# Gate projections of seven heads in a stage of their own, as seven products with eight sums

## The chip, the cores and the metric

The kernel runs on one core of a Trainium2 chip. The core has a matrix engine (TensorE, PE in the profile, with its weight loads as PEld), three engines for elementwise work (VectorE or DVE, ScalarE or ACT, GpSimd or POOL), a queue engine (SyncE or SP) and 16 DMA engines. All run their own instruction streams in order and wait for each other by semaphores. The metric is the device time of one execution in microseconds.

## The reference, cut to what matters

A block for 1024 tokens of width 1024: a normalization, one wide projection, a recurrent mixer with 8 heads of 128 (the part that is changed), an attention with 16 heads, two output projections that are gated and mixed, and a feed-forward part.

```python
h = rms_norm(x, norm1_gain[layer])
proj = h @ w_in[layer]
hq, hf, hi, hg, sq, sk, sv, ga, gb = split_cols(proj, IN_SPLITS)
o_hg = hgrn2_mixer(hq, hf, hi, lower_bounds[layer])
o_hg = rms_norm(o_hg, hg_out_norm[layer]).reshape(b, s, HG_WIDTH)
o_hg = o_hg * jax.nn.sigmoid(hg.astype(jnp.float32))
```

and in the mixer, for each head and in chunks of 64 tokens:

```python
f = lb + (1.0 - lb) * jax.nn.sigmoid(f_raw.astype(jnp.float32))
log_f = jnp.log(f)
k = 1.0 - f
...
cum = jnp.cumsum(g_c, axis=-2)
o = scores(q, k, cum) @ v + (q * exp(cum)) @ state
state = exp(last) * state + (k * exp(last - cum)).T @ v
```

The last two lines are shortened to their meaning. The two gate projections of a head are hf (the gate f) and hg (the output gate), each a product of a 1024 x 128 slice of w_in with h.

## The kernel before

**Exact products.** Each float32 operand is split into a rounded part and a rest (hi and lo, in a 32-bit format that PE reads in one pass). `mm3` (L158 to L162) makes one product of three matmuls: hi x hi, hi x lo, lo x hi. h is kept transposed as `hT[half][hi or lo]`, features on the partitions, 512 tokens in each half.

**Projections.** `proj_t` (through `chain`, L164) gives a 128-column slice of a projection, transposed: for each half, 8 steps over K, each an `mm3` with 512 columns, into a bank of the pool pd, and then an evacuation. `proj_v` gives tiles of v with 256-wide matmuls. Weights come by `load_w` (L121 to L141): a load on SP's queue into wr, a cast to wh on ACT, the negated copy to wl on ACT, and an accumulating DMA on POOL's queue that adds wr; for the first five loads the difference is made on DVE instead. wr has two buffers, wh and wl three each. `block` has the next two blocks loaded ahead.

**Start.** x comes in tiles of 128 tokens; `norm_x` normalizes a tile, `turn_x` transposes it on PE and splits it to hT. `first_head` gives the projections f, g and q of head 0: the first half of the tokens as quarters that are woven into the turning of the tiles (cut0, cut1), the second half behind it (rest). Then come the projections of v for heads 0 and 1 (v0).

**Recurrent stage.** For each of 8 heads, `hg_head` returns `prep` and a list of own steps with costs: `base` (scores in blocks of 4), `across`, four levels of scores (`level_prep` on DVE, POOL and ACT, `level` on PE and a predicated copy on DVE), `turn`, `state`, `read` and `norm`. `hg_gates` (L410 to L425) turns the projected f and g into gates: two Sigmoids on ACT, a table load before and one after, f = lb + (1 - lb) x on DVE, k on POOL, Ln on ACT, and a scan on DVE. The filling of head h is the projections f and g of head h+1 (`hg_fg`, with the gates behind them), q of head h+1, and two tiles of v; that of head 7 is three projections of other gates (`gate_steps`). `weave` fixes the order on PE: it lets filling go ahead by the cost `lead`, and spreads the rest over the own steps in proportion to their costs. PE's order is that of the program text; the other engines' orders are made by the planner from readiness and priority.

**Later stages.** The attention, the output projections and the feed-forward part follow. The last two use seven products in place of eight: both operands are cut in 2 x 2 quarters, sums and differences of quarters are made (`A_STEPS`, `B_STEPS`), and seven products of quarters are added up in banks and in SBUF. In the feed-forward part `a_prep` makes the weights' side six products ahead.

Of the kernel before, what the change touches and what calls it, by code (L numbers as in the profile page):

```python
# [41 lines left out]
def hybrid_block(ctx, tc, x, norm1_gain, w_in, lb_logits, hg_out_norm, sb_q_norm, sb_k_norm,  # L42
# [75 lines left out]
    d_x1 = dp.tile([NT, P, D], F32, name="d_x1")  # L118
    d_act = dp.tile([3, NF // 2, P, HS], F32, name="d_act")
# [99 lines left out]
    hg = hgctx.enter_context(tc.tile_pool(name="hg", bufs=2))  # L219
# [3 lines left out]
    g1 = hg.tile([P, D], F32, tag="sc", bufs=1, name="g1")  # L223
# [7 lines left out]
    xts = {}  # L231

    def fetch_x(t):
        xts[t] = hg.tile([P, D], F32, tag=("kv", "q")[t % 2], name="xt")
        nc.sync.dma_start(xts[t], x[t * P:(t + 1) * P, :])
        if t == 0:
            nc.sync.dma_start(g1, norm1_gain.partition_broadcast(P).rearrange("p a d -> p (a d)"))

    def norm_x(t):
        xt = xts.pop(t)  # L240
        hn = hg.tile([P, D], F32, tag=("c", "fv")[t % 2], name="hn")
        ss = mp.tile([P, 1], F32, tag="ss", bufs=8, name="ss")
        sq = nc.scalar.activation(hg.tile([P, D], F32, tag="ke", bufs=1, name="scr"), xt, AF.Square, accum_out=ss)
# [12 lines left out]
    def turn_x(t):  # L256
        hn, half, c0 = hns.pop(t), t // 4, (t % 4) * P
        for g in range(2):
            tp = pbank(("pt", "pz")[t % 2])
            for j in range(4):  # L260
                k = 4 * g + j
                nc.tensor.transpose(tp[:, j * P:(j + 1) * P], hn[:, k * P:(k + 1) * P], ident)
            last["hT"] = split_to(hT[half][0][:, 4 * g:4 * g + 4, c0:c0 + P],
                     hT[half][1][:, 4 * g:4 * g + 4, c0:c0 + P], tp.rearrange("p (k c) -> p k c", k=4))
# [8 lines left out]
    def small_vectors():  # L273
# [13 lines left out]
        nc.scalar.activation(lbt[:, 1:3, :], lbt[:, 1:3, :], AF.Exp)  # L287
# [85 lines left out]

    def first_head():
        d, cuts, rest = hd[0], ([], []), []
        for c0, n in ((1024, "fv"), (3072, "sg"), (0, "q")):
            w, evac = in_block(c0), copy_half(d, n)
            last.setdefault("w0", w)
            for a, b in zip(cuts, quarters(w, evac, n == "fv")):
                a.extend(b)  # L380
            rest += proj_t(w, evac, (1,))
            if n == "sg":
                rest.append((0.0, lambda: hg_gates(0)))
        return *cuts, rest

# [3 lines left out]
    def hg_v(h, tiles=range(4)):  # L389
        get = in_block(2048 + h * P, 256)  # L390
# [19 lines left out]

    def hg_gates(h):
        d = hd[h]
        fv, sg = d["fv"], d["sg"]
        with tc.high_priority():
            s1 = nc.scalar.activation(fv, fv, AF.Sigmoid)
# [3 lines left out]
        nc.vector.tensor_scalar(fv, fv, oml[:, h:h + 1], lb[:, h:h + 1], op0=ALU.mult, op1=ALU.add)  # L419
# [4 lines left out]
        order(nc.scalar.activation(c, fv, AF.Ln, bias=tiny), pre)  # L424
        nc.vector.tensor_tensor_scan(c, rmask, c, initial=0.0, op0=ALU.mult, op1=ALU.add)  # L425

    def hg_head(h):
# [5 lines left out]
        def prep():  # L433
            if h % 2 == 0:
# [3 lines left out]
            kb = e["kb"] = hg.tile([P, S], F32, tag="kl", name="kb")  # L438
            qb = e["qb"] = hg.tile([P, S], F32, tag="kl", name="qb")
# [6 lines left out]
            nc.vector.tensor_mul(kb, kb, kv)  # L446
# [6 lines left out]
            nc.vector.tensor_mul(ke, ke, kv)  # L453
# [60 lines left out]
        def level_prep(li):  # L514
            L = LEVELS[li]
            kq = hg.tile([P, 2, HS], F32, tag="kl", name="kq")
# [16 lines left out]
        def level(li):  # L533
# [3 lines left out]
            for a in range(NT // 2):  # L537
                sl = slice(a * P, (a + 1) * P)
                nc.tensor.matmul(ps[:, sl], kq[:, 0, sl], kq[:, 1, sl], start=True, stop=True)
            nc.vector.copy_predicated(bl(e["sc"], L)[:, :, 1, :],  # L540
                                      lmask[:, li, :].rearrange("p (b l) -> p b l", l=L),
                                      ps.rearrange("p (b l) -> p b l", l=L))
# [14 lines left out]
        def norm(half):  # L557
# [14 lines left out]
            (0.5, lambda: turn(0)),  # L572
            (1.257, lambda: turn(1)),
            (2.053, lambda: (level(1), level_prep(3))),
            (0.9, lambda: state(0)),
            (0.7, lambda: state(1)),
            (1.7, lambda: level(2)),
            (2.397, lambda: level(3)),
            (1.6, lambda: read(0)),
            (4.5, lambda: read(1)),  # L580
            (3.0, lambda: norm(0)),
            (0.45, lambda: norm(1)),
# [18 lines left out]
    v0 = hg_v(0)  # L601
# [22 lines left out]
    weave([(1.0, lambda t=t: turn_x(t)) for t in range(4, 8)], cut1, lead=3.429)  # L624
    hg_constants()
    small_vectors()
# [277 lines left out]
    def run(steps):  # L904
        for _, f in steps:
            f()

    A_STEPS = {5: (21, 21, 22, ALU.add), 6: (21, 21, 11, ALU.subtract), 7: (11, 22, 21, ALU.subtract),
               3: (12, 12, 21, ALU.subtract)}
    A_SRC = {1: 11, 2: 12, 5: 21, 6: 21, 7: 11, 3: 12, 4: 22}
    B_STEPS = {5: (11, 12, 11, ALU.subtract), 6: (11, 22, 11, ALU.subtract), 7: (12, 22, 12, ALU.subtract),
               4: (21, 21, 11, ALU.subtract)}
    B_SRC = {1: 11, 2: 21, 5: 11, 6: 11, 7: 12, 3: 22, 4: 21}
    INTO = {1: 11, 2: 11, 5: 22, 6: 12, 7: 22, 3: 12, 4: 21}
    OPENS, CHAIN = (1, 2, 5), (1, 6, 7, 4)
    FIRST, FINAL = (1, 5, 6, 4), (2, 7, 3, 4)

    def sum_step(e, steps, m, raw):
        if m in steps:
            to, a, b, op = steps[m]
            e.tensor_tensor(raw(to), raw(a), raw(b), op=op)  # L924

    def split(e, src, hi, lo):
        nc.scalar.copy(hi, src)  # L927
        e.tensor_sub(lo, src, hi.bitcast(F32))  # L928

    def chain_mm(ps, lhs, rhs, m, k, nk):  # L930
        mm3(ps, lhs, rhs, m in OPENS and k == 0, k == nk - 1, m not in OPENS)

# [233 lines left out]
    a_ops = {}  # L1166

    def a_prep(n):
        f, m = a_order[n]
        if m == 1:  # L1170
            load_raw(f)
        if m == 2:
            load_raw(f + 1)
        raw = lambda q: raws[f][q // 10 - 1][:, 4 * (q % 10) - 4:4 * (q % 10), :]
# [212 lines left out]
```

## Time and profile before

| | us |
|---|---|
| median of 3 runs (lowest, highest) | 2033.01 (2032.94, 2033.84) |
| the profiled execution | 2032.44 |
| its span, first to last instruction | 2030.6 |
| scan of head 0, of head 7 (L425) | 56.3, 460.0 |
| last predicated copy of head 7 (L540) | 500.0 |
| last store of the recurrence (L565) | 519.8 |

The scans of heads 0 and 7 lie 403.7 us apart, 57.7 us a head. The profile comes from one execution; its times are compared with each other and with its own 2032.44 us. In its rows a line such as "L342 DVE COPY fv<-pd 128x512 x2 | 1.4, 688 | 3.3 <-PE pd L162 3.3" means: line 342, engine, operation, tile written and tile read, shape, count, busy time in us, mean of one in ns, idle time of the engine ahead of it and what ended that. Rows of a timeline begin with the start and the duration.

### The profile page before, as it was taken

Reading aid. Unit: us, or ns where it says so; the run is one execution under the profiler, and the core shown is the slowest. Engines: PE = TensorE matmul, PEld = TensorE weight load, DVE = VectorE, ACT = ScalarE, POOL = GpSimd, SP = SyncE. Lnnn points to the kernel's source line nnn. Section 1 sums busy time; section 2 is a strip of 40 time slices with the busy share of each in tenths; the row PEclk is TensorE's granted clock in tenths of the full one; section 3 lists DMA queues with packets and bytes.
Section 4 is the critical chain, followed back from the end, with each engine's and each line's share of the span. In section 5 each row is a group of like instructions: output and inputs, shape, how many; then the busy total and the mean of one; then the engine's idle time right before and its main releaser. Section 6 shows DMA issues by size and latency. Waiting matters only on the chain.

```text
span 2030.6 us, 29534 instructions
## 1 busy us (share of the span) xinstructions
PE 2013.3 (99%) x11047; PEld 1727.5 (85%) x11047; DVE 1463.5 (72%) x2263; ACT 1131.6 (56%) x1889; POOL 322.1 (16%) x445
## 2 busy tenths in 40 slices
PE   9999999999999999999999999998999999999999
PEld 8988888888888988988988888887888888888887
DVE  6455666557277787787888598999766666568975
ACT  5455655455477777877877465458333333334443
POOL 1233323323231332232231000000000000000000
PEclk9999999999999999999999999999999999999999
DMA  4444434444555454444454644512322222266031
GB/s 166 115 110 109 115 94 125 113 127 104 132 114 115 97 127 114 99 108 113 104 118 112 229 170 162 182 49 98 103 81 86 83 81 65 78 221 221 30 114 42
DMA packets 204511, 234.74 MB, mean 116 GB/s; under 512 B 11416, under 2 KB 141904, under 8 KB 204368
## 3 DMA queue, kind: packets, MB, share of 16 engines
q1 hardware_dynamic: 181584, 185.01, 29.2%
q0 software_dynamic: 15632, 42.48, 12.1%
q10 hardware_dynamic: 7152, 5.37, 0.8%
q8 instruction: 87, 1.43, 0.3%
q14 instruction: 56, 0.46, 0.1%
HBM read 137.65 MB, written 42.21 MB: 89 GB/s over the span
## 4 chain that ended last, share of the span: by engine, by line
PE 86%; DVE 9%; ACT 1%; issue 1%; DMA 1%; POOL 0%; SPq 0%; DVEq 0%; ACTq 0%; POOLq 0%
PE pd L160 19%; PE pd L162 18%; PE pd L161 18%; PE pt L807 3%; PE pt L161 3%; PE pt L160 3%; PE pt L162 3%; DVE u L924 2%; PE po L824 2%; DVE u L928 2%; PE po L823 2%; PE pz L762 2%; PE pz L763 2%; PE po L160 2%; PE po L162 2%; PE po L161 2%
## 5 line engine op out<-in xcount | busy, mean ns | idle before, releaser
L160 PE MATMUL pd<-hT,wh 128*128 128x512 f32 (+1 forms) x912 | 368.6, 404 | 0.0
L162 PE MATMUL pd<-hT,wl 128*128 128x512 f32 (+1 forms) x912 | 352.7, 387 | 0.1
L161 PE MATMUL pd<-hT,wh 128*128 128x512 f32 (+1 forms) x912 | 352.4, 386 | 0.0
L927 ACT CAST wh<-u 128x512 fp32r<-128x512 f32 (+1 forms) x280 | 183.6, 684 | 227.0 <-PE po L162 86.6
L162 PEld LDWEIGHTS pd<-hT,wl 128*128 128x128 f32 x912 | 171.3, 188 | 36.6 <-DVE wl L138 0.3
L160 PE MATMUL pd<-u,wh 128*128 128x512 f32 x496 | 194.0, 391 | 1.5 <-ACT c L1235 0.7
L161 PE MATMUL pd<-u,wh 128*128 128x512 f32 x496 | 193.3, 390 | 0.2 <-DVE u L928 0.2
L160 PEld LDWEIGHTS pd<-hT,wh 128*128 128x128 f32 x912 | 172.0, 189 | 23.8
L161 PEld LDWEIGHTS pd<-hT,wh 128*128 128x128 f32 x912 | 172.2, 189 | 23.4 <-DVE hT L210 0.2
L928 DVE TENSOR_TENSOR wl<-u,wh 128x512 fp32r<-128x512 f32 (+1 forms) x196 | 150.3, 800 | 47.4 <-ACT wh L927 45.0
L774 DVE TENSOR_TENSOR_SCAN kp<-kp,dsel 128x512 f32<-128x512 f32 (+3 forms) x128 | 122.6, 958 | 36.6 <-ACT kp L767 36.0
L160 PE MATMUL pd<-wh,hT 128*128 128x256 f32 x512 | 148.0, 289 | 0.0
L162 PE MATMUL pd<-wh,hT 128*128 128x256 f32 x512 | 144.7, 283 | 0.0
L161 PE MATMUL pd<-wl,hT 128*128 128x256 f32 x512 | 144.6, 282 | 0.0
L767 ACT ACTIVATE kp<-pz,rq 128x128 f32<-128x128 f32 (+2 forms) x192 | 114.1, 594 | 44.0 <-PE pz L763 33.7
L162 PE MATMUL pd<-u,wh 128*128 128x512 f32 x352 | 137.0, 389 | 0.0
L924 DVE TENSOR_TENSOR u<-u,u 128x512 f32<-128x512 f32 (+1 forms) x152 | 124.3, 851 | 12.6 <-DMA u<-d_ohg 7.9
L810 DVE TENSOR_TENSOR tl<-pt,th 128x512 fp32r<-128x512 f32 (+1 forms) x160 | 100.1, 626 | 34.1 <-ACT th L809 33.7
L781 DVE TENSOR_TENSOR a<-a,kp 128x128 f32<-128x128 f32 (+2 forms) x192 | 109.7, 572 | 17.8 <-ACT a L767 3.4
L767 ACT ACTIVATE a<-pz,rq 128x128 f32<-128x128 f32 (+2 forms) x192 | 114.2, 595 | 7.2 <-PE pt L807 7.2
L160 PEld LDWEIGHTS pd<-u,wh 128*128 128x128 f32 x496 | 93.1, 188 | 21.7 <-ACT c L1235 1.1
L161 PEld LDWEIGHTS pd<-u,wh 128*128 128x128 f32 x496 | 93.2, 188 | 19.8 <-DVE u L928 0.9
(266 smaller groups left out, 4885.9 us busy)
## 6 DMA issues: line engine op xcount, KB each, us to landing
wr<-in_w_in SPq DMA_DIRECT2D x78, 512.0 KB, 4.0
wl<-wr POOLq DMA_DIRECT2D x73, 512.0 KB, 4.7
u<-in_w_ffn_in SPq DMA_DIRECT2D x24, 512.0 KB, 5.8
wr<-in_w_ffn_in SPq DMA_DIRECT2D x20, 512.0 KB, 3.9
u<-in_w_ffn_out SPq DMA_DIRECT2D x10, 1024.0 KB, 6.6
d_act<-c SPq DMA_DIRECT2D x33, 256.0 KB, 2.2
u<-d_act SPq DMA_DIRECT2D x8, 1024.0 KB, 13.3
qh<-qh SPq DMA_DIRECT2D x48, 128.0 KB, 2.3
```

Of the source, the lines that this page charges most:

```text
L160: nc.tensor.matmul(ps, lh, rh, start=start, stop=False, skip_group_check=adds)
L161: nc.tensor.matmul(ps, lh, rl, start=False, stop=False, skip_group_check=adds)
L162: nc.tensor.matmul(ps, ll, rh, start=False, stop=stop, skip_group_check=adds)
L762: nc.tensor.matmul(ps[:, :n], qhi[:, qs], kk[:, k0:k0 + n], start=True, stop=False)
L767: last["sig"] = [nc.scalar.activation(t[:, 0:w], ps[:, 0:w], AF.Sigmoid, scale=rq[:, n_, col:col + 1]) for n_, t in enumerate((kp, a))]
L774: nc.vector.tensor_tensor_scan(rev, rev, dsel[:, HS - w:][:, ::-1], initial=0.0, op0=ALU.mult, op1=ALU.max)
L781: nc.vector.tensor_mul(a[:, 0:w], a[:, 0:w], kp[:, 1:w + 1])
L807: nc.tensor.transpose(tp[:, s * P:(s + 1) * P], a[:, b * P:(b + 1) * P], ident)
L810: nc.vector.tensor_sub(tl[:, c0:], tp[:, c0:], th[:, c0:].bitcast(F32))
L924: e.tensor_tensor(raw(to), raw(a), raw(b), op=op)
L927: nc.scalar.copy(hi, src)
L928: e.tensor_sub(lo, src, hi.bitcast(F32))
```

## The change

The projections f and g of heads 1 to 7 leave the recurrent stage. They are made ahead of it in a stage of their own. For each head the weights (columns of f and of g as the two halves of the output, two halves of K) and h (two halves of K, two of the tokens) are cut in quarters, and seven products of 128 x 512 x 512 give the four quarters of the result. The sums on h's side are made once for all heads; those on the weights' side once for each head. The results go through Sigmoid, those of f through their scale and bound, and are stored to DRAM (d_fg). The recurrent stage loads them back (`hg_load`). Its filling is now q and v alone, heads 6 and 7 get one and two of the other gate projections, the own steps' order and costs are other ones, and there is a buffer count of 4 for kl. A class that was the feed-forward part's loop (`Pairs`) serves both stages.

```diff
+    class Pairs:
+        def prep(self, n):
+            f, m = self.order[n]
+            self.before(f, m)
+            raw = lambda q: self.raws[f][q // 10 - 1][:, 4 * (q % 10) - 4:4 * (q % 10), :]
+            both = wp.tile([P, 2, 4, P], F32R, tag=("wh", "wl")[n % 2], name="wh")
+            sum_step(nc.vector, A_STEPS, m, raw)
+            split(nc.vector, raw(A_SRC[m]), both[:, 0], both[:, 1])
+            self.ops[f, m] = both
+            self.after(f, m)
...
+        def step(self, n, k):
...
+            if k == 0:
+                self.ahead(n + 6)
...
+            chain_mm(ps, (w[:, 0, k, :], w[:, 1, k, :]), (bh[:, k, :], bl_[:, k, :]), m, k, 4)
+            if k == 3:
+                del self.ops[f, m]
+                self.done(f, m, ps)
...
+            last["hT"] = split_to(hT[half][0][cut], hT[half][1][cut], tp)
+            nc.scalar.copy(h_raw[q][:, :, c0:c0 + P], tp)
...
-    def hg_fg(h):
-        d = hd[h]
-        f, g = in_block(1024 + h * P), in_block(3072 + h * P)
-        return proj_t(f, copy_half(d, "fv")) + proj_t(g, copy_half(d, "sg")) + [(0.0, lambda: hg_gates(h))]
...
+    def to_gate(h, i, half, dst, src):
+        last["sig0"] = nc.scalar.activation(dst, src, AF.Sigmoid)
+        order(last["sig0"], last["rs", NT - 1], last["lb"])
+        if i == 0:
+            nc.vector.tensor_scalar(dst, dst, oml[:, h:h + 1], lb[:, h:h + 1], op0=ALU.mult, op1=ALU.add)
+        nc.sync.dma_start(d_fg[i][h][:, half * HS:(half + 1) * HS], dst)
...
+    h_sums = [lambda: h_sum(11, 12, 11), lambda: h_sum(12, 22, 12), lambda: h_sum(22, 22, 11), lambda: h_split(5, 11),
+              lambda: h_split(6, 22), lambda: h_sum(22, 21, 22), lambda: h_split(7, 12), lambda: h_split(4, 22)]
...
+    def hg_load(h):
+        d = hd[h]
+        for i, name in enumerate(("fv", "sg")):
+            d[name] = hg.tile([P, S], F32, tag=name, bufs=i + 1, name=name)
+            nc.sync.dma_start(d[name], d_fg[i][h])
...
     def hg_gates(h):
         d = hd[h]
-        fv, sg = d["fv"], d["sg"]
-        with tc.high_priority():
-            s1 = nc.scalar.activation(fv, fv, AF.Sigmoid)
-            order(s1, last[id(d), "sg"])
-            s2 = nc.scalar.activation(sg, sg, AF.Sigmoid)
-            pre = exp_ln_tables(s1, s2)
-        nc.vector.tensor_scalar(fv, fv, oml[:, h:h + 1], lb[:, h:h + 1], op0=ALU.mult, op1=ALU.add)
+        fv = d["fv"]
...
-            nc.vector.tensor_mul(kb, kb, kv)
+            order(nc.vector.tensor_mul(kb, kb, kv), *last.get("own", ()))
...
-            (0.86, lambda: (base(0), load_v(h) if h % 2 == 0 else None)),
-            (2.463, lambda: (base(1), level_prep(0))),
-            (2.075, lambda: (across(), level_prep(1))),
-            (2.243, lambda: (level(0), level_prep(2))),
...
+            (0.86, lambda: (base(0), load_v(h) if h % 2 == 0 else None, level_prep(0),)),
+            (2.46, lambda: (base(1), level_prep(1),)),
+            (5.60, lambda: (across(), level_prep(2),)),
+            (2.24, lambda: (level(0), level_prep(3),)),
...
-    weave([], rest + v0)
+    for i, (_, f) in enumerate(rest):
+        f()
+        if i % 3 == 2 and i < 14:
+            h_sums.pop(0)()
+        if i % 8 == 7:
+            pairs0.ahead(2 * (i // 8 + 1))
+    n0 = len(pairs0.order)
+    for n in range(n0):
+        if n == n0 - 5:
+            get = in_block(2048, 256)
+            get()
+            v0 = [hg_v(0, tiles, get) for tiles in ((0, 1), (2, 3))]
+        weave([], pairs0.steps(n))
+        if h_sums:
+            h_sums.pop(0)()
+    s0ctx.close()
+    hg = hgctx.enter_context(tc.tile_pool(name="hg", bufs=2, reuse_waits="tile"))
+    last["tables"] = [exp_ln_tables(last["sig0"])]
+    hg_load(0)
+    hg_gates(0)
+    weave([], v0[0])
+    prep, own = hg_head(0)
+    prep()
+    weave([], v0[1])
...
     for h in range(NH):
-        prep, own = hg_head(h)
-        prep()
         if h < NH - 1:
-            fill = hg_fg(h + 1) + hg_q(h + 1)
+            fill = hg_q(h + 1) + [(0.0, lambda: hg_gates(h + 1))]
+            if h == NH - 2:
+                fill += gate_steps(1)
             if h < NH - 2:
                 fill += hg_v(h + 1, (2, 3)) if h % 2 else hg_v(h + 2, (0, 1))
         else:
-            fill = gate_steps(3)
-        weave(own, fill, lead=6.109)
+            fill = gate_steps(2)
+        load_blocks()
+        if h > 0:
+            prep, own = hg_head(h)
+            prep()
+        if h < NH - 1:
+            hg_load(h + 1)
+        weave(own, fill, lead=5.53)
```

`h_sum` makes a difference of two quarters of h on DVE in two pieces of 128 x 1024, `h_split` a cast on ACT and a difference on DVE of such a quarter. `pair_done` copies the first part of a quarter of the result from its bank on ACT, adds the second on DVE, and passes it to `to_gate`. `pair_raw(f)` loads the weights of one head, 512 KB for f and 512 KB for g.

More of the change, by code (lines that the diff above doesn't have):

```diff
@@ new lines, in hybrid_block, with sum_step, split, chain_mm @@
+    OPENS, CHAIN = (1, 2, 5), (1, 6, 7, 4)
+    FIRST, FINAL = (1, 5, 6, 4), (2, 7, 3, 4)
+    def sum_step(e, steps, m, raw):
+        if m in steps:
+            to, a, b, op = steps[m]
+            e.tensor_tensor(raw(to), raw(a), raw(b), op=op)
+    def split(e, src, hi, lo):
+        nc.scalar.copy(hi, src)
+        e.tensor_sub(lo, src, hi.bitcast(F32))
+    def chain_mm(ps, lhs, rhs, m, k, nk):
+        mm3(ps, lhs, rhs, m in OPENS and k == 0, k == nk - 1, m not in OPENS)
+    class Pairs:
+        def __init__(self, order, raws, bop, before, after, done):
+            self.order, self.raws, self.bop = order, raws, bop
+            self.before, self.after, self.done = before, after, done
+            self.ops, self.banks, self.ready = {}, {}, 0
+        def prep(self, n):
[7 more added lines that the diff above has]
+            self.after(f, m)
+        def ahead(self, upto):
+            while self.ready < min(upto, len(self.order)):
+                self.prep(self.ready)
+                self.ready += 1
+        def step(self, n, k):
+            f, m = self.order[n]
+            key = f, "p" if m in CHAIN else "t"
+            if k == 0:
+                self.ahead(n + 6)
+                if m in OPENS:
+                    self.banks[key] = dbank() if m == 1 else pbank("po", 1) if m == 2 else pbank("pt")
+            ps, w = self.banks[key], self.ops[f, m]
+            bh, bl_ = self.bop[m]
+            chain_mm(ps, (w[:, 0, k, :], w[:, 1, k, :]), (bh[:, k, :], bl_[:, k, :]), m, k, 4)
+            if k == 3:
+                del self.ops[f, m]
+                self.done(f, m, ps)
+        def steps(self, n):
+            return [(0.65, lambda k=k: self.step(n, k)) for k in range(4)]
@@ new lines, in piece, with evac, go @@
+    def piece():
+        return s0.tile([P, HS], F32, tag="c", bufs=6, name="c")
+    postponed = []
+    def first_head():
+        cuts, rest = ([], []), []
+        def evac(i):
+            def go(half, ps):
+                c = piece()
+                if i == 2:
+                    nc.vector.tensor_copy(c, ps)
+                    nc.sync.dma_start(d_q[:, half * HS:(half + 1) * HS], c)
+                elif half == 1:
+                    to_gate(0, i, half, c, ps)
+                else:
+                    nc.vector.tensor_copy(c, ps)
+                    postponed.append(lambda: to_gate(0, i, half, c, c))
+            return go
+        for i, c0 in enumerate((1024, 3072, 0)):
+            w = in_block(c0)
@@ L386, in hg_q, with pair_order, hg_v @@
+    def pair_order(n_pairs, ahead):
+        order = [(f, m) for f in range(ahead) for m in (1, 2)]
+        for f in range(n_pairs):
+            n = [(f + 1, m) for m in (1, 2)] if ahead <= f + 1 < n_pairs else []
+            order += [(f, 5), (f, 6)] + n[:1] + [(f, 7)] + n[1:] + [(f, 3), (f, 4)]
+        return order
+    pairs0 = Pairs(pair_order(NH - 1, 2), raws0, hop, lambda f, m: None,
+                   lambda f, m: pair_raw(f + 2) if m == 4 else None, pair_done)
     def hg_q(h):
         return proj_t(in_block(h * P), copy_half(hd[h], "q"))
-    def hg_v(h, tiles=range(4)):
-        get = in_block(2048 + h * P, 256)
+    def hg_v(h, tiles=range(4), get=None):
+        get = get or in_block(2048 + h * P, 256)
@@ L906, in run @@
             f()
[L911 to L931, printed above, removed]
     def four_banks(m):
@@ L1318, in hybrid_block @@
             load_w_out(11, 0, unit2)
-        run(ffn_in(n))
+        run(ffn.steps(n))
     for i, u in ((1, unit1), (2, unit1)):
```

188 lines of the change are left out of this document (112 added, 76 removed).

## The prediction

> **What bounds the kernel now.** I read the page's busy shares and slices first, then the busy times in stretches of the span, then the waits of PE, and last the groups of one head.
>
> ```profile
> span 2030.6 us, 29534 instructions
> PE 2013.3 (99%) x11047; PEld 1727.5 (85%) x11047; DVE 1463.5 (72%) x2263; ACT 1131.6 (56%) x1889; POOL 322.1 (16%) x445
> PE   9999999999999999999999999998999999999999
> DVE  6455666557277787787888598999766666568975
> PE pt L1122 <- DVE hn L1118: 5.5, 1, 5.5
> PE pz L539 <- DVE kq L529: 1.1, 1, 1.1
> ```
>
> PE has work in every slice, and its list of waits holds two above 1.4 us in the whole span; neither falls in the stage that the change empties, except the second, in head 7. So PE's issue bounds the kernel nearly everywhere, and a matmul removed is worth its issue interval, not its printed duration: matmuls overlap in the pipeline. The interval is read where nothing but 512-wide matmuls runs, and from the first and last of a run of 256-wide ones.
>
> ```profile
> core 0: us, PE busy (x) PEld busy (x) DVE busy (x) ACT busy (x) POOL busy (x), PEclk, DMA share, GB/s
> 1600.00:1700.00 100.00, 100.00 (x443) 82.84 (x442) 63.90 (x96) 36.77 (x63) 0.00 (x0) 1.00 0.24 72
> 287.80:345.50 57.70, 57.70 (x362) 50.93 (x362) 35.26 (x54) 31.48 (x44) 18.02 (x18) 1.00 0.51 125
> 352.07 0.28 PE L160 MATMUL pd<-wh,hT 128*128 128x256 f32 x1
> 357.82 0.28 PE L160 MATMUL pd<-wh,hT 128*128 128x256 f32 x1
> ```
>
> 443 matmuls in 100 us give 0.2257 us for a 512-wide one. Between the two single rows lie 48 issues in 5.75 us, 0.12 us for a 256-wide one. The third row is one head of the recurrent stage, 57.7 us long: PE never idle, DVE 61%, ACT 55%, POOL 31%.
>
> The head takes apart so: the gates f and g are 2 x 2 halves x 8 x 3 = 96 matmuls, 21.7 us; q is 48, 10.8 us; two tiles of v are 96 narrow ones, 11.5 us. The recurrence's own PE work is the rest, 57.7 - 44.0 = 13.7 us. Own work waits for DVE and ACT at each step, and the 44 us of projections hide those waits.
>
> **The change, part by part.**
>
> *Products.* Seven products x 4 steps x 3 matmuls are 84 where 96 stood: 12 x 0.2257 = 2.71 us less per head, and 7 x 2.71 = **19.0 us** less PE time in all. No other PE work goes or comes: the gate steps of heads 6 and 7 are three as before, split one and two. If nothing stalls, the time falls by 19.0 us; there is no second saving on PE, so this is the end of the range.
>
> *The new stage.* 49 products x 12 x 0.2257 = 132.7 us of PE. Beside it, DVE and ACT have this work, priced by the rows of the same kind of work in the feed-forward part:
>
> ```profile
> L928 DVE TENSOR_TENSOR wl<-u,wh 128x512 fp32r<-128x512 f32 (+1 forms) x196 | 150.3, 800 | 47.4 <-ACT wh L927 45.0
> L924 DVE TENSOR_TENSOR u<-u,u 128x512 f32<-128x512 f32 (+1 forms) x152 | 124.3, 851 | 12.6 <-DMA u<-d_ohg 7.9
> L927 ACT CAST wh<-u 128x512 fp32r<-128x512 f32 (+1 forms) x280 | 183.6, 684 | 227.0 <-PE po L162 86.6
> ```
>
> Per head DVE has 7 differences (5.6), 4 sums (3.4), 3 additions and 2 gate steps (2.8): 11.8 us in 19.0. ACT has 7 casts (4.8) and 7 copies or sigmoids of 0.54, half of the 1.08 us rows below (3.8): 8.6 us. The row 1600 to 1700 above is this scheme running with PE full, so I price the steady stage at no wait. Its loads are two of 512 KB per 19 us; they sit in SP's queue behind the stores of finished gates, and have three products (8 us) until their first cast and six more until PE.
>
> *Its start.* The eight sums over h (19 us of DVE, at 1.2 us for 128x1024) and the preparation of the first products are new on DVE just as hT is finished, and 16 raw copies (0.54 us each) are new on ACT before it.
>
> ```profile
> 34.83 1.08 ACT L209 CAST hT<-pt 128x512 fp32r<-128x512 f32 x2 [1.22 <-PE pt L262]
> 36.77 1.07 ACT L209 CAST hT<-pz 128x512 fp32r<-128x512 f32 x2 [0.87 <-PE pz L262]
> 37.73 1.27 DVE L210 TENSOR_TENSOR hT<-pz,hT 128x512 fp32r<-128x512 f32 x2
> 38.93 0.68 DVE L342 COPY q<-pd 128x512 f32<-128x512 f32 x1
> 45.00 1.23 DVE L138 TENSOR_TENSOR wl<-wr,wh 128x1024 fp32r<-128x1024 f32 x1 [0.17 <-ACT wh L135]
> ```
>
> hT is whole at 39.0 us, and PE wants its second K half about 41.3: 2.3 us of slack, against copies on ACT that fit its gaps here (0.9 to 1.2 us each) but push each cast by some half a microsecond. From 39.5 on, PE has 16.2 us of head 0's second half and 10.8 us of four products that need no sum. By the first use of the last sum, DVE has 19 us of sums, 9 differences (7.2), 4 weight sums (3.4) and some 6 of evacuations and small vectors: 36 us, and PE reaches that use after 16.2 + 8 x 2.7 = 37.8 us. I take **2 us** of PE wait. The ends are 0 (it fits as counted) and 8 us (waits on casts cost DVE 10 of the 37.8 us), and 2 is the nearer to the count.
>
> *The passage to the recurrence.* Nothing of the new pool can be filled until the stage's last tiles are free; then come a load, Ln, the scan, POOL's difference, Exp and two multiplications:
>
> ```profile
> wr<-in_w_in SPq DMA_DIRECT2D x78, 512.0 KB, 4.0
> 342.99 2.29 DVE L425 TENSOR_TENSOR_SCAN c<-rmask,c 128x1024 f32<-128x1024 bf16 x1
> 345.44 1.89 POOL L441 TENSOR_TENSOR qb<-c 128x1024 f32<-128x1024 f32 x1 [2.23 <-DVE c L425]
> 347.36 1.15 ACT L444 ACTIVATE kb<-qb 128x512 f32<-128x512 f32 x2 [1.81 <-POOL qb L441]
> 348.61 1.80 DVE L446 TENSOR_TENSOR kb<-kb,kv 128x1024 f32<-128x1024 f32 x1 [1.26 <-ACT kb L444]
> ```
>
> That is 3 (last gate and its store) + 4.0 + 1.1 + 2.3 + 1.9 + 1.2 + 1.8 and 2.3 for qb: about 18 us. PE has v of heads 0 and 1 in the meantime, 192 x 0.12 = 23 us, and the lead of 5.53 (5.8 us). Priced at nothing; without that cover it would be the 18 us.
>
> *The recurrence with less filling.* Per head PE keeps q, v and its own work: 10.8 + 11.5 + 13.7 = **36.0 us**. The other engines lose this:
>
> ```profile
> L342 DVE COPY fv<-pd 128x512 f32<-128x512 f32 x2 | 1.4, 688 | 3.3 <-PE pd L162 3.3
> L419 DVE TENSOR_SCALAR fv<-fv,lbt 128x1024 f32<-128x1024 f32 x1 | 0.8, 812 | 0.0
> L122 ACT ACTIVATE wl<-wr 128x1024 fp32r<-128x1024 f32 x5 | 5.3, 1061 | 1.7 <-PE pd L161 1.7
> L135 ACT CAST wh<-wr 128x1024 fp32r<-128x1024 f32 x5 | 5.2, 1048 | 0.0
> L415 ACT ACT_TABLE_LOAD x1 | 1.3, 1283 | 0.0
> L123 POOL DMA_DIRECT2D wl<-wr x5 | 4.4, 882 | 10.7 <-ACT wl L122 6.0 <-DVE qe L482 4.7
> ```
>
> DVE loses four copies and the gate step: 35.3 - 2.8 - 0.8 = 31.7 us, **88%** of 36.0. ACT loses two of five weight splits (4.2), two sigmoids (2.1) and two table loads (2.6): 22.6 us. POOL loses two DMA issues: 16.3 us. SP gains two loads of 512 KB per head, asked for a head ahead, into buffers that are free by then. The weights of v come into buffers freed at the end of the previous head's filling, some 14 us before use; the path load, cast, difference, accumulating DMA is 4 + 2 + 1 + 5 = 12 us, the load ahead of time.
>
> So DVE becomes nearly the bound, and the question is how much PE waits at 88%. Head 7 of before is the nearest row: its filling is thin already, and between its first and last scores DVE was as full as that.
>
> ```profile
> 478.10:500.70 22.60, 22.60 (x140) 19.01 (x139) 19.89 (x38) 8.78 (x12) 6.29 (x6) 1.00 0.59 153
> ```
>
> DVE 19.89 of 22.6 us, 88%, PE full; the 1.1 us on L539 is all that head 7's levels cost there. The change helps this stretch: with four kl buffers two of the four levels can be prepared before the first scores. That moves 5.6 of some 24 us of DVE work out of a stretch that shrinks to about 18.6 us of PE. The added order (kb and ke wait for the last level's scores) holds back what stands behind them on DVE, but 15 us remain until the next head's first scores. The lower end is 0; the upper end is 4 us a head (the stretch keeps its 22.6 us). I take **0.7 us**, between 0 and head 7's 1.1, nearer the latter since eight heads in a row can't borrow from a denser neighbour: 8 x 0.7 = 5.6 us.
>
> *Sum.* The profiled execution took 2032.44 us (span 2030.6 and 1.8 around it). 2032.4 - 19.0 + 2 + 5.6 = 2021.0; the median of the runs is 0.6 above that execution, so **2021.5 us**.
>
> **Rivals.** *No stall at all*: 2033.0 - 19.0 = 2014. For it: the 22.6 us stretch without a gap. Against: DVE at 88% for 290 us in a row.
>
> *DVE paces the heads.* DVE idles 57.7 - 35.3 = 22.4 us a head now. If 6.3 of that stays because its queue waits in order for scores, Exp and the norm, a head takes 31.7 + 6.3 = 38 us: 2 us lost on each, 16 + 2 back of 19, 2032, no change.
>
> ```profile
> L563 DVE SCALAR_TENSOR_TENSOR r<-pt,cols,r 128x512 f32<-128x512 f32 x2 | 1.5, 750 | 7.3 <-ACT r L562 7.3
> L467 DVE COPY_PREDICATED sc<-bmask,pz 128x512 f32<-128x512 uint8 x2 | 1.5, 734 | 3.1 <-PE pz L465 3.1
> ```
>
> For it: 10.4 us of the present idle time stand at just such waits. Against: DVE had nothing else to do in them then.
>
> *DVE and POOL take turns* (slower). The rows of one shape show that DVE stretches where POOL works beside it:
>
> ```profile
> L523 DVE TENSOR_TENSOR kq<-c x64: 410/427/1381, 88.7 to 493.7; 128x256 f32<-128x256 f32 x64
> L485 DVE TENSOR_TENSOR eb<-el x8: 400/1565/1702, 58.9 to 465.7; 128x8 f32<-128x8 f32 x8
> ```
>
> ```profile
> L523 DVE TENSOR_TENSOR kq<-c 128x256 f32<-128x256 f32 x8 | 5.1, 689 | 0.0
> L437 POOL MEMSET sc<- 128x1024 f32 x1 | 1.0, 955 | 2.4 <-issue 2.4
> ```
>
> The 128x256 difference takes 0.41 us at best and 1.38 at worst, a 128x8 product mostly 1.57 us. In the head of before the eight differences had a mean of 0.69. Undisturbed, DVE's head would be 8 x 0.28 + 1.17 = 3.4 us shorter, 28.3; POOL's reading, without its DMA issues and the memset, is 16.3 - 2.6 - 1.0 = 12.7. One after the other they need 41.0 us, 5.0 more than PE's 36.0: 40 + 2 - 19 = 23 us slower, 2056. It decides from 38.4 us a head on, where eight stalls of 2.4 eat the 19 us. Against it: from 478.1 to 500.7 DVE and POOL together were busy 26.2 us in 22.6, so much of it does overlap. The Trainium skill, "SBUF — State Buffer", section "Who interferes with whom", has a rule that speaks for this rival: a DVE instruction with two SBUF inputs and a GpSimd instruction that reads SBUF exclude each other for the whole of one. By that rule 2056 would be the time if every DVE instruction were of that kind; the trace agrees for the rows above, and copies from PSUM and predicated copies are not of that kind.
>
> *A long wait slows the clock.* One wait of 5.5 us is in the trace, and the five microseconds behind it ran at 0.66:
>
> ```profile
> 1400.00:1405.00 5.00, 3.94 (x14) 3.38 (x15) 5.00 (x9) 2.13 (x4) 0.00 (x0) 0.66 0.02 3
> ```
>
> That is 1.7 us on top of a wait of that length; at the start or the passage a wait of 5.5 would cost 7.2 in place of 2, and the time be 2027. I count it with the forecast's upper part.
>
> **How the numbers follow.** A measurement of this kernel can tell about 0.2% (4 us) from no change. No stall (2014 to 2016): 0.12. Forecast (2016 to 2029): 0.60. DVE paces (2029 to 2037): 0.16. Turns (above 2037): 0.12. Faster is 0.72, same 0.16, slower 0.12. The range leaves out the turns and little else: 2014 to 2036.
>
> **What would show it.** 84 matmuls of 512 columns fewer; the new stage about 133 us with 443 matmuls in 100 us; heads of 36 to 37.5 us between scans, with DVE at 84 to 88% and PE's new waits on kq, sc or kb; at most a few microseconds of PE wait on hi, lo or wh near 40 to 80 us. The forecast is wrong if heads are above 38 us, if PE waits at the passage for v or kb, or if weights of q and v come late. The turns are shown by mean durations of the level differences (L523 before) well above 0.69 us.

## The result and the profile after

| | us |
|---|---|
| before, median of 4 runs (lowest, highest) | 2033.38 (2032.94, 2033.84) |
| after, median of 4 runs (lowest, highest) | 2057.03 (2053.37, 2058.82) |
| ratio, with its 95% interval | 1.0114 (1.0096, 1.0132) |
| the profiled execution after, its span | 2053.37, 2051.3 |

The change makes the kernel 1.1% slower, where 0.6% faster was predicted. The profile after is of the fastest of its four runs, 3.7 us below their median. The page of the changed kernel shows first that the work went away as counted, and then what came in its place:

```profile
span 2051.3 us, 29673 instructions
PE 2006.9 (98%) x10963; PEld 1720.6 (84%) x10963; DVE 1522.5 (74%) x2355; ACT 1141.7 (56%) x1957; POOL 318.4 (16%) x431
PE   8999899999999999999999999998999999999999
PE pd L231 14%; PE pd L232 14%; PE pd L233 14%; DMA d_vr<-d_v 3%; PE pt L1011 3%; PE pt L233 3%; PE pt L231 3%; PE pt L232 3%; PE po L1028 2%; PE po L231 2%; PE po L1027 2%; PE po L232 2%; PE po L233 2%; PE pz L966 2%; PE pz L967 2%
```

10963 matmuls are 84 fewer than 11047. In the chain that ended last stands a piece that the chain of before has not: the transfer `d_vr<-d_v`, 3% of the span. It is the copy within DRAM that turns every odd tile of v upside down (turn_v, L564), which then comes back to SBUF (load_v, L568). The waits of PE name the same place (line waited at, releaser, then total us, times, longest):

```profile
PE pt L667 <- ACT ket L658: 13.8, 5, 8.4
PE pt L667 <- DMA v<-d_vr: 3.3, 4, 1.0
PE pt L715 <- DVE sc L703: 2.5, 3, 1.1
PE pd L232 <- DMA wl<-wr: 1.7, 2, 0.9
PE pz L390 <- DVE sql L385: 1.3, 3, 0.4
```

L667 is the first product with v in the step `state`. 17.1 us of PE's new wait stand there. The waits of before had nothing at that line. ACT, named first, is only the messenger. That is shown by the chain of work of the first pair of heads (start, duration, what), and by ACT's timeline of the second pair:

```profile
227.26 0.27 ACT vs L557
...
231.67 12.96 DMA d_vr<-d_v
244.63 0.02 issue
244.66 2.84 DMA v<-d_vr
247.50 0.04 issue
247.54 1.65 PE pt L667 x6
```

```profile
323.78 0.93 ACTq L568 DMA_DIRECT2D v<-d_vr  x2
324.75 0.97 ACT L658 COPY ket<-pt 128x512 f32<-128x512 f32 x2 [7.48 <-DMA d_vr<-d_v]
```

ACT's queue stood 7.48 us at the issue of the load, which waits for the copy; the copies of ket stand behind it in ACT's order; and PE waits for ket. From the last tile of v (227.26) to the state step (247.54) the chain is 20.3 us. Before, the copy took as long, but had more room, as the issues of its first pair show, with the first state product of head 0 behind them:

```profile
82.81 1.19 ACTq L404 DMA_DIRECT2D d_vr<-d_v  x1
94.91 0.95 ACTq L408 DMA_DIRECT2D v<-d_vr  x2
105.66 1.05 PE L504 MATMUL pt<-v,ket 128*128 128x128 f32 x8
```

That is 12.1 us from copy to load, and 22.9 us from copy to use. The waits also cost clock. Busy times by stretch (PE, PEld, DVE, ACT, POOL, each with its count, then granted clock, DMA share, GB/s) of three pairs:

```profile
240.00:250.00 10.00, 3.26 (x13) 2.97 (x14) 1.01 (x4) 4.36 (x7) 1.88 (x3) 0.56 0.28 90
320.00:330.00 10.00, 6.04 (x37) 5.48 (x36) 6.15 (x11) 5.25 (x8) 4.40 (x6) 0.83 0.53 155
400.00:410.00 10.00, 6.71 (x37) 6.35 (x38) 5.18 (x10) 6.25 (x9) 3.77 (x5) 0.75 0.59 164
```

PE is idle for much of these stretches and works at a lower clock behind the waits. Finally the milestones: where the projections of v begin, after and before, and the last store of the recurrence after.

```profile
L232 PEld LDWEIGHTS pd<-wl,hT x512: 186/192/333, 194.8 to 1016.2; 128*128 128x128 f32 x171
L161 PEld LDWEIGHTS pd<-wl,hT x512: 187/192/192, 54.8 to 996.4; 128*128 128x128 f32 x171
L730 SPq DMA_DIRECT2D d_ohg<-r x16: 319/320/338, 269.5 to 539.3; - x16
```

v begins at 194.8. Before, it began at 54.8, and with 132.7 us of the new stage it would be 187.5. So start and stage lose 7.3 us. The last store is at 539.3 where it was at 519.8, so 19.5 of the span's 20.7 us arise ahead of it, although 19.0 us of work have gone there.

The span takes apart so. PE's idle time is 2051.3 - 2006.9 = 44.4 us, before 2030.6 - 2013.3 = 17.3: 27.1 more, of which 17.1 are the waits for v, 5.5 the other three rows of the table, and the remaining 4.5 lie mostly in the start. PE's busy time fell by 6.4 us where 19.0 us of work are gone: the same work took 12.6 us longer. Some 7.6 us of that are the lower clock behind the waits: in steps of 1 us, PE's busy time times what the clock lacked of 1.00 adds up to 9.0 us, before to 1.4. The rest isn't taken apart. 27.1 - 6.4 is the 20.7.

### The profile page after: what moved, and what is told of

It is laid out like the page before. It is cut to its first block, busy times and chain, and to the rows that moved or that the text cites. A ratio compares the mean times of both kernels' runs of the same rounds, so it can differ in the third digit from the quotient of the medians.

```text
span 2051.3 us, 29673 instructions
## 1 busy us (share of the span) xinstructions
PE 2006.9 (98%) x10963; PEld 1720.6 (84%) x10963; DVE 1522.5 (74%) x2355; ACT 1141.7 (56%) x1957; POOL 318.4 (16%) x431
## 4 chain that ended last, share of the span: by engine, by line
PE 71%; DVE 9%; DMA 4%; issue 2%; ACT 2%; POOL 1%; DVEq 0%; POOLq 0%; ACTq 0%
PE pd L231 14%; PE pd L232 14%; PE pd L233 14%; DMA d_vr<-d_v 3%; PE pt L1011 3%; PE pt L233 3%; PE pt L231 3%; PE pt L232 3%; PE po L1028 2%; PE po L231 2%; PE po L1027 2%; PE po L232 2%; PE po L233 2%; PE pz L966 2%; PE pz L967 2%
## 5 line engine op out<-in xcount | busy, mean ns | idle before, releaser
L231 PE MATMUL pd<-hT,wh 128*128 128x512 f32 (+1 forms) x716 | 286.7, 400 | 0.0
L232 PE MATMUL pd<-hT,wh 128*128 128x512 f32 (+1 forms) x716 | 276.0, 385 | 0.5 <-DVE hT L281 0.5
L233 PE MATMUL pd<-hT,wl 128*128 128x512 f32 (+1 forms) x688 | 264.9, 385 | 0.0
L231 PE MATMUL pd<-wh,hT 128*128 128x256 f32 x512 | 153.6, 300 | 0.0
L233 PEld LDWEIGHTS pd<-hT,wl 128*128 128x128 f32 x688 | 129.2, 188 | 26.9
L232 PEld LDWEIGHTS pd<-hT,wh 128*128 128x128 f32 x716 | 135.2, 189 | 18.7 <-DVE hT L281 0.9
L231 PEld LDWEIGHTS pd<-hT,wh 128*128 128x128 f32 x716 | 135.0, 189 | 18.2
L233 PE MATMUL pd<-wh,hT 128*128 128x256 f32 x512 | 145.6, 284 | 0.0
```

What stands on the lines that cost most here:

```text
L231: nc.tensor.matmul(ps, lh, rh, start=start, stop=False, skip_group_check=adds)
L232: nc.tensor.matmul(ps, lh, rl, start=False, stop=False, skip_group_check=adds)
L233: nc.tensor.matmul(ps, ll, rh, start=False, stop=stop, skip_group_check=adds)
```

## The experiments

Theory A was that the turning copy is the loss. The rival B was that DVE, nearly full in the shorter heads, paces them, so that another wait takes its place. Ratios are against the kernel before, timed on the same chip, with 95% intervals.

**The copy taken away.** The first kernel leaves the turning out, so that odd tiles of v are in unturned order; the second does the same to the kernel before.

```diff
     def turn_v(h):
-        nc.scalar.dma_start(d_vr[h // 2], d_v[h // 2, :, ::-1, :])
+        pass
...
-                                d_vr[h // 2, :, :, j * P:(j + 1) * P].rearrange("a p c -> p a c"))
+                                d_v[h // 2, :, :, j * P:(j + 1) * P].rearrange("a p c -> p a c"))
```

> The changed kernel without the turning copy d_vr<-d_v: the odd tiles of v are loaded from d_v directly, in the unturned order of tokens. Theory A (PE waits in the even heads for the odd tiles of v, whose turning copy takes some 13 us and starts only when the last tile of v is stored): the four long waits at the state step (18.5 us of idle PE between 230 and 485 us) shrink to a few us, the clock stays at 1.00, and the time falls from 2057 to about 2027. Theory B (DVE and POOL take turns, PE waits for DVE): the copy is no part of it, the time stays above 2045.

> The kernel before without the turning copy d_vr<-d_v (odd tiles of v loaded in unturned order). Theory A: with 57.7 us a head the 12 us of the copy lie under the filling, so nothing changes: 2031 to 2035. If the copy itself cost time (DMA bandwidth, ACT's queue), this kernel too would be faster by some us.

Measured: 2040.1 us, 1.0032 (1.0020, 1.0044), for the changed kernel, and 2032.86 us, 0.9993 (0.9983, 1.0002), for the kernel before. So the copy cost nothing before and about 17 us (2057.0 - 2040.1) after. But 2040 is 13 above the 2027 of A: a second loss lay behind the first. The waits that are left say at which lines:

```profile
PE pt L715 <- DVE sc L703: 7.9, 6, 2.6
PE pt L667 <- ACT ket L658: 4.4, 3, 2.8
```

**Whose queue?** ACT's queue stands at the load of v. If that were the harm, issuing the load from SP would mend it:

```diff
     def load_v(h):
         for j in range(2):
-            nc.scalar.dma_start(hd[h + j]["v"][:, 1::2, :],
+            nc.sync.dma_start(hd[h + j]["v"][:, 1::2, :],
```

> The changed kernel with the loads v<-d_vr issued on SP's queue instead of ACT's, the copy left as it is. Theory A1 (the data of v is late): the state step waits for v itself at the same time, 2050 to 2058. Theory A2 (ACT's queue stands still behind the load that waits for the copy, and with it the ket copies and Exps): PE's waits fall by more than half, 2030 to 2040.

> The changed kernel without the turning copy and with the loads of v on SP's queue. After e1 (2040) two theories stand for what is left: A2, ACT's queue still stands behind the loads of v, which wait for the last store of v, and Exps and DVE with it: then 2026 to 2032. B2, DVE and its partners are too full in the thin heads (waits on sc L703): then 2037 to 2041 again.

Measured: 2057.78 us, 1.0119 (1.0104, 1.0134), with the copy kept; 2043.31, 1.0044 (1.0027, 1.0060), with the copy out as well.

```profile
PE pt L667 <- DMA v<-d_vr: 17.7, 4, 10.0
```

With ACT free, PE waits just as long, 17.7 us, now for the data itself. The queue was the messenger; the cause is the chain with the copy's 12 to 13 us in it. With the copy out, SP's queue was no help either: 2043 is above both ranges that were expected, with 7.0 us of wait for ket and 7.6 for sc.

**Four ways to start the copy earlier, all worse or no better.** Two halves of the copy, each behind its two tiles; v before q in every second head, with the copy right behind it; the same with v's weights prepared once for two heads; and that with more lead in head 0 and the load on SP.

```diff
-    def turn_v(h):
-        nc.scalar.dma_start(d_vr[h // 2], d_v[h // 2, :, ::-1, :])
+    def turn_v(h, g):
+        nc.scalar.dma_start(d_vr[h // 2, g:g + 2], d_v[h // 2, g:g + 2, ::-1, :])
```

> The changed kernel with the turning copy cut in two, each half issued right behind its two tiles of v. Theory A: only 256 KB are left to turn after the last tile, some 6 us less of each of the four waits, and less slow clock: 2032 to 2042. Theory B: no change, 2053 to 2058.

```diff
+                if h % 2:
+                    fill = hg_v(h + 1, (2, 3)) + [(0.0, lambda: turn_v(h + 1))] + fill
...
```

> The changed kernel with the two tiles of v ahead of q in the filling of the odd heads, and the turning copy right behind them. Theory A: the copy starts some 11 us earlier for heads 2, 4 and 6, their waits (8.7 us of idle PE and some 5 of slow clock) go, head 0's stays: about 2043. Theory B: no change or slower, since the gates of the next head come later.

```diff
+            if h % 2 and h < NH - 2:
+                fill = hg_v(h + 1, (2, 3), get) + [(0.0, lambda: turn_v(h + 1)), (0.0, lambda: hg_gates(h + 1))]
+                fill += hg_q(h + 1)
...
```

> The changed kernel with v ahead of q in the odd heads, the turning copy right behind v, and the weights of v kept from the even head (loaded once for four tiles instead of twice). Theory A: heads 2, 4 and 6 get v some 11 us earlier and lose their waits, and the weights that came late in e4 are there already; head 0 keeps its wait: 2036 to 2044. If e4's loss was not the late weights but the place of v or of the gates, this one stays above 2060.

```diff
-        weave(own, fill, lead=5.53)
+        weave(own, fill, lead=5.53 if h else 15.0)
```

> e7 with a lead of 15.0 instead of 5.53 in head 0, and the loads of v on SP's queue. Theory A: head 0's state step comes some 10 us later on PE, so its wait for v goes too; its levels run with less filling and give back 2 to 5 us: 2026 to 2034.

| | us | ratio | largest waits of PE, us |
|---|---|---|---|
| halves | 2080.14 | 1.0228 (1.0211, 1.0245) | weights wl 34.2 |
| v first | 2100.16 | 1.0321 (1.0305, 1.0338) | weights wl 29.6, ket 12.7 |
| v first, shared weights | 2059.70 | 1.0127 (1.0106, 1.0148) | ket 12.9, sc 8.0 and 4.0 |
| the same, lead and SP | 2063.82 | 1.0145 (1.0130, 1.0160) | sc 9.3 and 7.8 |

None came into the range that theory A expected. The first two put the wait onto v's weights, which now came too late; the third mended that (no wait on wl is left), but put the gates behind v, and the wait went to the scores, while 8.8 us of the wait on ket stayed with the first pair. Shifting a 20 us chain about in a 36 us head moved the wait from one consumer to the next.

**No chain through DRAM.** v's odd tiles come out of PE in turned order if PE's stationary operand, the columns of hT, is turned. ACT copies those columns in reverse order (hR) ahead of the projection; the stores, the copy and the loads of v are gone. The load of sg goes into the head that uses it.

```diff
+                [hR[tp][:, t, k, :] if turned and j else hT[half][t][:, k, c0:c0 + P] for t in range(2)],
...
+    def turned_h(tiles):
+        for tp in tiles:
+            hR[tp] = hg.tile([P, 2, KT, P], F32R, tag="hR", bufs=2, name="hR")
+            half, c0 = tp // 2, (2 * tp + 1) % 4 * P
+            for t in range(2):
+                nc.scalar.copy(hR[tp][:, t], odd(hT[half][t][:, :, c0:c0 + P]))
...
-            vs = hg.tile([P, 2 * P], F32, tag="vs", name="vs")
-            nc.scalar.copy(vs, ps[:, 2 * P:])
-            nc.sync.dma_start(d_v[h // 2, tp], vs)
```

> The changed kernel with v's odd tiles turned without DMA: ACT copies h of an odd tile in reversed order of tokens ahead of v's matmuls (4 copies of 128x1024 a head, some 4.2 us of ACT), and v comes out turned; the stores, the turning copy and the loads of v are gone. Theory A (the chain through DRAM was late): as in e1 the long waits at the state step go, 2036 to 2044, head 0 included since nothing of v passes through DRAM. If the waits of e1 come from ACT being late, ACT's added copies make them longer: 2044 to 2050.

> e9 with the weights of v kept from the even to the odd head (loaded and split once for four tiles): ACT has 4.2 us less and POOL two DMA issues less in each odd head. If late ACT and POOL are what is left, 3 to 8 us faster than e9; if DVE alone paces the thin heads, the same as e9 within 2 us.

> e10 with the two evacuations of q per head on ACT instead of DVE: DVE has 1.4 us less a head, of some 32. If DVE paces the thin heads (waits on sc at the read step), these waits go and it is 4 to 8 us faster than e10; if ACT does, it is as much slower.

Measured: 2037.96 us, 1.0022 (1.0011, 1.0033); with v's weights shared by two heads 2037.49, 1.0019 (1.0009, 1.0028); with q's evacuations on ACT as well 2050.74, 1.0087 (1.0070, 1.0104). In the first the scans of DVE stand at even distances:

```profile
278.08 2.28 DVE L593 TENSOR_TENSOR_SCAN c<-rmask,c 128x1024 f32<-128x1024 bf16 x1
314.80 2.28 DVE L593 TENSOR_TENSOR_SCAN c<-rmask,c 128x1024 f32<-128x1024 bf16 x1
351.56 2.28 DVE L593 TENSOR_TENSOR_SCAN c<-rmask,c 128x1024 f32<-128x1024 bf16 x1
```

A head is 36.7 us from scan to scan, as predicted (36.0 and 0.7 of wait). The sum of ACT's work is not the limit: sharing takes casts off ACT and changes nothing. Taking q's copies off DVE made it worse, by 13 us. What is left is one wait a head, at the read step, on the levels' scores. DVE's own timeline shows why those are late:

```profile
284.34 1.23 DVE L613 TENSOR_TENSOR qb<-qb,q 128x1024 f32<-128x1024 f32 x1 [2.04 <-ACT qb L611]
285.48 0.34 DVE L677 SCALAR_TENSOR_TENSOR st<-st,eb,pt 128x128 f32<-128x128 f32 x1
285.74 0.70 DVE L706 COPY_PREDICATED sc<-lmask,pz 128x512 f32<-128x512 uint8 x1
```

and in PE's timeline and its list of waits:

```profile
287.44 0.68 PE L718 MATMUL pt<-sc,v 128*128 128x128 f32 x4 [1.07 <-DVE sc L706]
```

```profile
PE pt L718 <- DVE sc L706: 8.7, 7, 2.6
```

DVE stands idle 2.04 us at a multiplication of the next head (qb by q) that waits for ACT, while states and scores of this head are queued behind it. With q's copies on ACT, this idle time doubles:

```profile
287.38 1.23 DVE L613 TENSOR_TENSOR qb<-qb,q 128x1024 f32<-128x1024 f32 x1 [4.12 <-POOL kq L690]
```

Heads are 39 to 40 us there. POOL is named, but ACT's exponential of qb ends only at 287.28, behind one of ke that itself waits 2.26 us for POOL. So this chain comes later in that kernel, and its time says nothing of DVE's or ACT's sums. The change orders the multiplications of kb and ke behind the last level's copy, but not that of qb.

**The missing order.** One line, in the kernel without the DRAM chain, in the one with shared weights, and in the changed kernel itself:

```diff
-            nc.vector.tensor_mul(qb, qb, q)
+            order(nc.vector.tensor_mul(qb, qb, q), *last.get("own", ()))
```

> The kernel of e9 with one more order: the multiplication of qb by q on DVE waits, like those of kb and ke, for the last level's predicated copy. Theory (what is left over the sum of e9 is the order on DVE: qb's multiplication waits 2.04 us for ACT ahead of the level copies, and PE waits 1.06 us a head at the read): those waits go, 7 x 1.06 + 2.65 of head 7 and some 2 of slow clock, 2025 to 2030 us, heads of 36.0 us between scans, and faster than the kernel before. Rival (DVE's load of 88% itself costs it, wherever the multiplication stands): the waits come back at kb's own scores or at sc, no change, 2035 to 2040.

> The kernel of e10 (v's weights prepared once for two heads) with the same order for qb. If ACT's or POOL's load matters once the order is right, it is faster than e12 by over 2 us; if not, equal within 2 us.

> The changed kernel itself with qb's multiplication ordered the same way, the turning copy of v kept. Theory (the copy's waits at the state step are a separate loss of some 17 us and 10 of slow clock): 2050 to 2057, its waits on ket and v stay above 12 us in all. Rival (the order was behind those waits too): below 2045.

Measured: 2025.22 us, 0.9956 (0.9942, 0.9969); 2024.54, 0.9949 (0.9936, 0.9961); and 2049.96, 1.0080 (1.0066, 1.0094). The first:

```profile
PE pt L718 <- DVE sc L706: 1.7, 5, 0.4
```

```profile
275.57:311.32 35.75, 35.40 (x265) 32.76 (x264) 29.20 (x48) 26.03 (x38) 17.93 (x15) 1.00 0.53 133
```

The wait of 8.7 us is 1.7, the head from scan to scan 35.75 us, and DVE 29.2 of that (82%). DVE no longer waits ahead of qb. Both kernels are faster than the kernel before, and they lie within 2 us of each other, so ACT's load doesn't matter once the order is right. In the changed kernel the same line is worth 7 us by the medians (3.8 us by the last store of the two profiles, 539.3 and 535.5), while its waits for ket and v stay at 14.3 + 3.7 us: two separate losses; the time is at the lower edge of what was expected.

**The start.** The last question was what makes the start dearer than predicted. On the kernel with shared weights, POOL makes the raw h from its two parts in place of 16 copies on ACT; then the copies are left out altogether, with the sums over the high parts, so that products 4 to 7 leave out the low part of h.

```diff
-            nc.scalar.copy(h_raw[q][:, :, c0:c0 + P], tp)
+            nc.gpsimd.tensor_add(h_raw[q][:, :, c0:c0 + P], hT[half][0][cut].bitcast(F32), hT[half][1][cut].bitcast(F32))
```

> The kernel of e13, with the raw h of the start made by POOL as the sum of its two parts in place of 16 copies on ACT (POOL has nothing else to do from 10 to 40 us). Theory (the start's loss is the 16 copies of 0.59 us on ACT, which put the norms of the next tiles off, so that PE waits for hn and h_raw): PE's busy time in the first 50 us comes up from 43.98 to about 46 of 50, and the time falls by 2 to 4 us, to 2021 to 2023. Rival (the start is bound by DVE's eight sums from 44 us on, which this leaves, or POOL's sums stretch DVE's work beside them): 2024 to 2027, and PE waits as long, for DVE's hn or for h_raw's sums.

```diff
-            nc.scalar.copy(h_raw[q][:, :, c0:c0 + P], tp)
...
+        a, b = (h_raw[q] if q in h_raw else hT[q % 10 - 1][0][:, 4 * (q // 10) - 4:4 * (q // 10), :].bitcast(F32)
+                for q in (a, b))
```

> The kernel of e13 without the 16 copies of the raw h, on any engine: the eight sums read the high parts of hT, so the products of four to seven leave out the low part of h. Theory (the 16 copies on ACT make the start's excess): PE busy 46 or more of the first 50 us against 44.4 in e13, 2020 to 2022.5 us. Rival (DVE's eight sums and their place make it): 44 to 45 of 50, 2023 to 2026.

Measured: 2030.56 us, 0.9984 (0.9975, 0.9993), and 2022.06 us, 0.9946 (0.9933, 0.9960). The first is above both ranges expected of it: there the first sum of h began at 48.5 us, with 1.4 us of wait for POOL's own sums, where it began at 43.0 with the copies on ACT. The busy times from 40 to 80 us of the second show DVE full without the copies too; the start of v follows:

```profile
40.00:50.00 10.00, 10.00 (x48) 8.08 (x47) 10.00 (x17) 6.33 (x10) 4.34 (x3) 1.00 0.60 179
50.00:60.00 10.00, 10.00 (x46) 8.29 (x45) 10.00 (x14) 6.57 (x9) 3.22 (x4) 1.00 0.26 98
60.00:70.00 10.00, 10.00 (x46) 8.26 (x45) 10.00 (x14) 5.99 (x9) 0.00 (x0) 1.00 0.14 52
70.00:80.00 10.00, 8.35 (x37) 6.58 (x36) 9.38 (x15) 4.08 (x7) 0.00 (x0) 1.00 0.43 131
```

```profile
L232 PEld LDWEIGHTS pd<-wl,hT x384: 187/192/193, 194.1 to 986.8; 128*128 128x128 f32 x192
```

Without the copies PE has 45.02 us of work in the first 50 in place of 44.38, and gives it back from 50 to 100 (48.35 in place of 48.84). v begins at 194.1, with the copies at 194.3. So the milestone speaks for the rival, that DVE's queue of sums and splits bounds the start: work that comes earlier is given back in a wait of 1.65 us between 70 and 80. That wait is for a copy out of a bank on ACT; ACT had stood 2.59 us at a cast that waits for a sum on DVE, with the copy behind it in its order. No run changed DVE's sums or that order, so the bound is argued and not shown. The median is 2.5 us lower, in the range of the theory, but the intervals of the two ratios overlap nearly whole and the milestone doesn't move; whether the copies cost anything later stays open.

## Why the prediction was wrong, and where it was right

- **The step that failed** is that of the recurrence with less filling. Of the queues it listed q's and v's weights and SP's two loads, and it priced what PE waits for as DVE's load alone. The chain of v, store, turning copy, load, was not in it, although its rows stood in the trace before: 12.1 us from copy to load, and 22.9 us from copy to use, under a head of 57.7 us. In a head of 36 us the same chain is late. It costs 17.1 us of wait, and the clock behind it; without the copy the kernel was 17 us faster. The same step left out a second wait, at DVE's order around qb: the one line that mends it was worth 12.7 us in the kernel without the chain. That q and v alone are left as filling was priced as less cover for DVE; it also brought the last tile of v nearer to its use.
- **How much each is of the miss** follows from the stretch between the first matmul of v and the last store. Before, it is 465.0 us; less the 672 matmuls of f and g (151.7 us) that is 313.3 without a new stall, and the prediction added 5.6 for the eight heads.

| | from v to the last store, us | above 313.3 |
|---|---|---|
| the changed kernel | 344.5 | 31.2 |
| without the chain through DRAM | 327.5 | 14.2 |
| and with the order of qb | 315.6 | 2.3 |

So the chain is 17.0 us of it and the order 11.9. With the 7.3 us of start and stage and 1.2 us behind the last store, 31.2 + 7.3 + 1.2 - 19.0 is the 20.7 by which the span grew. The change also put the own steps in another order and gave kl four buffers; no run takes these apart.

- **Products**: 84 matmuls fewer, as counted; the stage ran at 222 matmuls in 50 us, with one wait of 0.7 us near its end.
- **The head's length**: in the changed kernel two pairs of heads took 79.0 and 80.3 us between scans, 40 us a head, above the 38 that were named as a sign against the forecast. Without the chain it is 36.7 us against 36.0 + 0.7, but that agreement is luck. The 0.7 was put down to a full DVE; the runs showed an order in its place, and with qb behind the level copies the head is 35.75 us. It also holds between scans only: in head 7 the same order cost 2.65 us of wait, and the clock behind it. DVE's 31.7 us a head was too high, 29.2 were measured.
- **Start and stage** were mis-sized: 2 us predicted, 7.3 measured. The count had hT whole at 39.0 us and then 36 us of DVE work against 37.8 us of PE. In the changed kernel hT was whole at 42.9 us, the first sum of h began behind it, and DVE was full from 40 to 70 us and 93% busy from 70 to 80:

```profile
43.52 1.22 DVE L494 TENSOR_TENSOR h_raw<-h_raw 128x1024 f32<-128x1024 f32 x1
```

So DVE's work was about as long as counted, and began some 4 us late. Of PE's 4.1 us of added idle time in the first 80 us, 2.8 lie in the first 40, where PE waits 1.8 us for DVE's hn (before 0.7) and 1.2 us for a raw copy. Without those copies hT was still whole only at 42.2 us; what else delays it wasn't tested.

- **The passage** was right: PE is full from 188 to 230 us of the changed kernel, and no wait on kb is in its list. The weights were late by 1.7 us in all. The wait of 8.4 us for v in head 0 comes after the passage and belongs to the chain.
- **A reading** was wrong without effect: PE's list of waits before holds one above 1.4 us, not two; the one in head 7 is 1.1.
- **The rivals.** The turns of DVE and POOL gave 2056, and 2057 came, but that is chance, not its mechanism: the mark set for it, level differences well above 0.69 us, didn't show.

```profile
L686 DVE TENSOR_TENSOR kq<-c 128x256 f32<-128x256 f32 x16 | 10.1, 688 | 0.0
```

That is the mean in two denser heads of after (288 to 369 us), equal to 689 before; over all heads it is 702, before 712. A long wait slowing the clock was right as a mechanism, but in other places, and with much shorter waits too. With the chain out and the order in, the kernel stands at 2025.2 for a forecast of 2021.5. There start and stage lose 8.0 us (v begins at 195.5), 6.0 more than predicted, and the recurrence loses 2.3, 3.3 less than predicted.

## What to carry to other kernels

Shortening a stage shortens the cover of every chain that runs beside it: list each transfer issued in the stage, with its time from issue to landing and from issue to use, and compare both with the new length, also where the change doesn't touch it. Where an engine named as releaser had itself been standing at a DMA issue, look at what that DMA waits for before moving the issue to another queue. And where urgent work is ordered on an engine, order every instruction of the next step behind it, not most of them.

## What the hardware showed beyond that

**A copy within DRAM took three times as long as a load of its size.** The turning copy of 512 KB (512 rows of 1 KB, in reverse order) took 12.96 us from its issue, where the median load of 512 KB of weights to SBUF takes 4.0. No run tells apart what makes it slow: DRAM as the target, the reverse order, or something else.

**Several short waits slow the clock too.** In the stretch from 400 to 410 us no wait of PE is above 2.2 us:

```profile
400.18 0.36 PE L232 MATMUL pd<-wl,hT 128*128 128x256 f32 x1 [0.81 <-DMA wl<-wr]
404.39 0.49 PE L667 MATMUL pt<-v,ket 128*128 128x128 f32 x2 [2.13 <-ACT ket L658]
405.85 1.65 PE L667 MATMUL pt<-v,ket 128*128 128x128 f32 x6 [0.98 <-DMA v<-d_vr]
```

and yet the mean clock was 0.75 there. Read in steps of 1 us, the clock is not reduced a little: it is 1.00 up to 405 us and 0.50 from there to 411. In the stretch from 240 to 250 us it is 0.50 from about 241.2 on, which is 3.3 us behind PE's last matmul. The Trainium skill, "TensorE: Matmul & The Clock Gate", section "What's actually happening", puts the half rate behind an idle window of some 3.4 us. The fall at 241.2 agrees; the one at 405 came when PE had been idle for 2.3 us of the last 3.4, in two pieces, which by that rule alone wouldn't have been enough.

**POOL's sums stretched some of DVE's two-input instructions.** Where POOL made the raw h, the normalization of x on DVE (two inputs in SBUF) took up to 1749 ns in place of 754 at most, and POOL's own sum 2264 at most and 1261 at least. The medians on DVE hardly differ, 748 and 744. Minimum, median and maximum, first with POOL beside it, then without:

```profile
L335 DVE SCALAR_TENSOR_TENSOR hn<-xt,rs,g x16: 744/748/1749, 7.2 to 41.7; 128x512 f32<-128x512 f32 x16
L352 POOL TENSOR_TENSOR h_raw<-hT,hT x16: 1261/1293/2264, 12.9 to 48.4; 128x512 f32<-128x512 f32 x16
```

```profile
L335 DVE SCALAR_TENSOR_TENSOR hn<-xt,rs,g x16: 741/744/754, 7.1 to 39.3; 128x512 f32<-128x512 f32 x16
```

That is the rule of the Trainium skill, "SBUF — State Buffer", section "Who interferes with whom", which the prediction named for the recurrence: here, in the start, the trace agrees. The kernel was 6 us slower (2030.56 for 2024.54); how much of that is the stretching, and how much the wait for POOL's slower sums, wasn't tested.
